# First norm by halves of the channels, two column tiles begun between the halves, and silu(c) rows by an identity product

## The chip, the cores and the metric

The kernel runs on one core of one Trainium2 chip. The metric is the device time of one execution in microseconds. TensorE (PE in the rows; PEld is its weight load), VectorE (DVE), ScalarE (ACT), GpSimd (POOL) and SyncE (SP, which issues most DMAs) each run their own queue of instructions in order.

## The reference

Two layers of a decoder trunk on 256 tokens of 1024 channels, in float32. What matters here is the head of each layer:

```python
mod = silu(c) @ w_ada[l] + b_ada[l]                    # 1024 -> 6 x 1024
sh1, sc1, gate_mix, sh2, sc2, gate_ffn = split(mod, 6)
h = rms_norm(x, norm_g[l, 0]) * (1.0 + sc1) + sh1
p = h @ w_in[l] + b_in[l]                              # 1024 -> 5144 columns
```

The columns of `p` feed an RWKV-7 time mix of 8 heads and a sparse attention of 8 heads; both are merged, projected and added to `x` with `gate_mix`. A second modulated norm (`sh2`, `sc2`) feeds a grouped top-2 mixture of 16 experts of width 512, added to `x` with `gate_ffn`.

## The kernel before

Activations lie transposed: `xT` holds 8 tiles of 128 channels by 256 tokens. The program is traced in Python, and a list scheduler orders each engine's queue at compile time by the order of tracing (the priority) and by its own estimate of when inputs are ready; on the chip each queue then runs in that fixed order, with semaphores.

**Start.** Ahead of the loop over layers, `x`, the vectors `v` and the constants' identity matrix are loaded. `cs` = silu(c) as a column of 8 per partition, `csx` its copy repeated 32 times. The sum of squares of `x` goes through ScalarE (L302), VectorE (L304) and TensorE (L307) to 1/rms (L245, L185), and `rs_rows` (L259) spreads it to rows in PSUM with a product against the identity. Then four pieces of the modulation of layer 0 are made in the order `ci` = 2, 0, 3, 1 (2 and 3 are the halves of `sc1`, 0 and 1 those of `sh1`): two weight tiles of 1 MB each (L313, `load` at L160) from a pool of eight, 8 products (16 instructions, L315), a copy by ScalarE (L318), four small products that sum the partitions back to a column (L321) and the sum with the bias (L322).

**Norm.** `norm_gain` makes `G` = (1 + sc1) * g in two operations (L252), and `norm_apply` goes over the 8 channel tiles: VectorE multiplies `xT`, `G` and the rows (L268), ScalarE adds the shift and rounds to the high part `h2[0]` (L269), VectorE makes the low part `h2[1]` (L270).

**Projection.** The input projection goes by column tiles of 128. `proj` takes a weight tile from a ring of three (`wcol`, 256 columns, so two column tiles each), splits its 1024 floats per partition into a high part (ScalarE, L274) and a low part (VectorE, L275), in one of two pairs of buffers, and `mm3` (L288) makes 24 products: for each channel tile high x high and low x high, then high x low. ScalarE takes the sum out of PSUM twice (L415, L417), and VectorE mixes it with the token before (L418). The tiles (0, 0) and (0, 128) come first, then those of the head pairs (`channels`, from weight tile 1 on).

**Rest of the mixing part.** The steps of the RWKV heads, the attention and the remaining modulation follow in a list written by hand (`STEPS`). The remaining modulation pieces (8 of this layer and 4 of the next) are reductions on VectorE: each of four operations per piece multiplies a loaded tile `wa` (L223) with `crow`, the row silu(c) in every partition, and sums (L225). `crow` is loaded in each layer, broadcast over the partitions, behind the first column tile; four pieces of it go through ScalarE (L431) and GpSimd (L432, L433).

**Experts.** 192 expert weight tiles of 1 MB in all are loaded through rings whose buffers come free as the mixing part and the experts before them finish. In layer 1 the rows of 1/rms come from the end of layer 0's experts, and the first half of the modulation is there already.

**Constants.** The rest of the constants `C` and the mask table `R` are loaded behind the modulation: a one-element copy from `mod` into the tile (L325, L355) holds the load back.

## Time and profile before

| | |
|---|---|
| timed runs | 1196.70, 1196.71, 1189.70 us; median 1196.7 |
| profiled execution | 1189.87 us, of which the span of the profile is 1188.1 |
| busy | PE 1068.4, PEld 688.4, DVE 653.2, ACT 402.8, POOL 134.1 us |
| TensorE clock granted, mean of the span | 0.959 |
| HBM read | 325.98 MB, 275 GB/s over the span |

Times in rows are microseconds from the start of the span, unless marked ns. The profiled execution's own time is longer than its span by what lies around the span.

### The profile page before, as it was taken

How to read it: one execution, taken by the hardware profiler on the slowest of the kernel's cores; microseconds unless marked ns; L12 is line 12 of the kernel's file. 1: busy time of each engine (PE TensorE's matmuls, PEld its weight loads, DVE VectorE, ACT ScalarE, POOL GpSimd, SP SyncE). 2: the span in 40 equal slices, each digit the busy share in tenths (PEclk: the TensorE clock that was granted, in tenths of full speed). 3: DMA queues.
4: the chain of work that ended last, by engine and by line, in shares of the span. 5: the costliest groups of instructions: out<-in, count | busy, mean ns of one | idle time of the engine just before them, and what ended most of it. 6: DMA issues, size and time to landing. Idle time of an engine off the chain costs nothing. (4 is left out here: it accounts for less than half of the span.)

```text
span 1188.1 us, 19652 instructions
## 1 busy us (share of the span) xinstructions
PE 1068.4 (90%) x7568; PEld 688.4 (58%) x7568; DVE 653.2 (55%) x1727; ACT 402.8 (34%) x922; POOL 134.1 (11%) x196
## 2 busy tenths in 40 slices
PE   5779899998797999999968999999989799999996
PEld 2658767886696343333337777778769744333432
DVE  1799788788575322121238988886748532212222
ACT  1634434356553020101035444344655321120100
POOL 0431232310000000000023212331000000000000
PEclk9889999999798999999988899999999899999998
DMA  9755664474577999999775466433346969999991
GB/s 382 266 189 187 224 226 174 168 245 164 200 311 321 373 421 419 420 420 419 295 268 179 152 239 213 161 135 133 108 167 273 409 267 420 420 420 419 419 396 38
DMA packets 52815, 328.48 MB, mean 276 GB/s; under 512 B 5856, under 2 KB 7520, under 8 KB 18784
## 3 DMA queue, kind: packets, MB, share of 16 engines
q1 hardware_dynamic: 52416, 326.91, 70.5%
q8 instruction: 63, 1.03, 0.3%
q14 instruction: 48, 0.39, 0.1%
q10 hardware_dynamic: 288, 0.14, 0.0%
HBM read 325.98 MB, written 1.05 MB: 275 GB/s over the span
## 5 line engine op out<-in xcount | busy, mean ns | idle before, releaser
L288 PE MATMUL ps_mm<-h,w 128*128 128x256 f32 x1824 | 266.8, 295 | 16.4 <-ACT w L274 8.1
L288 PEld LDWEIGHTS ps_mm<-h,w 128*128 128x128 f32 x1824 | 233.5, 194 | 35.7 <-issue 10.1
L275 DVE TENSOR_TENSOR w<-w,w 128x1024 fp32r<-128x1024 f32 (+2 forms) x130 | 140.2, 1082 | 16.3 <-ACT w L274 16.1
L274 ACT ACTIVATE w<-w 128x1024 fp32r<-128x1024 f32 (+2 forms) x130 | 120.1, 936 | 61.4 <-PE ps_mm L288 36.7
L1353 PE MATMUL ps_mm<-w,xeA 128*64 128x512 f32 x512 | 130.1, 599 | 0.0
L1364 PE MATMUL ps_mm<-w,hb 128*64 128x512 f32 (+1 forms) x576 | 123.0, 607 | 1.7 <-DMA w<-in_exp 1.2
L225 DVE CUSTOM_DVE_ANT_0 wa<-wa,crow 128x1024 f32<-128x1024 f32 x80 | 98.3, 1229 | 1.2 <-DMA wa<-in_ada 1.0
L1353 PE MATMUL ps_mm<-w,xeB 128*32 128x512 f32 (+1 forms) x640 | 97.8, 595 | 0.0
L275 DVE TENSOR_TENSOR ys<-ps_mm,ys 128x512 fp32r<-128x512 f32 x28 | 19.2, 686 | 110.5 <-ACT ys L274 110.5
L1364 PEld LDWEIGHTS ps_mm<-w,hb 128*64 128x64 f32 (+1 forms) x576 | 36.6, 127 | 73.3 <-issue 66.3
L737 PE MATMUL ps_mm<-w,h 128*128 128x512 f32 (+1 forms) x288 | 76.2, 394 | 1.0 <-DVE w L275 0.7
L1353 PEld LDWEIGHTS ps_mm<-w,xeA 128*64 128x64 f32 x512 | 37.5, 137 | 65.6 <-issue 62.3
L1307 DVE SCALAR_TENSOR_TENSOR hb<-hb,ps_mm 128x256 f32<-128x256 f32 x28 | 11.8, 421 | 99.7 <-ACT hb L1306 99.7
L274 ACT ACTIVATE ys<-ps_mm 128x512 fp32r<-128x512 f32 x28 | 16.7, 596 | 131.2 <-PE ps_mm L1364 101.3
L1308 DVE SCALAR_TENSOR_TENSOR hb<-ps_mm,sw,hb 128x256 f32<-128x256 f32 x28 | 12.3, 480 | 86.5 <-PE ps_mm L1353 86.5
L1329 DVE SCALAR_TENSOR_TENSOR xT<-ps_rw,gfh,xT 128x256 f32<-128x256 f32 x112 | 46.6, 478 | 23.3 <-PE ps_rw L1326 23.3
L1353 PEld LDWEIGHTS ps_mm<-w,xeB 128*32 128x32 f32 (+1 forms) x640 | 26.0, 115 | 51.8 <-issue 48.4
L737 PEld LDWEIGHTS ps_mm<-w,h 128*128 128x128 f32 x288 | 48.1, 198 | 12.5 <-issue 2.7
L1326 PEld LDWEIGHTS ps_rw<-ohT,ys 128*128 128x128 f32 x224 | 30.6, 188 | 38.8 <-ACT ys L274 19.4
L1243 PEld LDWEIGHTS ps_rw<-OH,h 128*128 128x128 f32 x256 | 35.7, 208 | 29.7 <-issue 23.8
L288 PE MATMUL ps_mm<-y,w 128*128 128x256 f32 x384 | 49.8, 294 | 3.2 <-ACT w L274 3.0
L288 PEld LDWEIGHTS ps_mm<-y,w 128*128 128x128 f32 x384 | 48.9, 200 | 3.9 <-ACT w L274 3.8
(458 smaller groups left out, 1512.9 us busy)
## 6 DMA issues: line engine op xcount, KB each, us to landing
w<-in_exp SPq DMA_DIRECT2D x192, 1024.0 KB, 19.7
w<-in_win SPq DMA_DIRECT2D x40, 1024.0 KB, 4.9
wa<-in_ada SPq DMA_DIRECT2D x80, 512.0 KB, 4.5
w<-in_ada SPq DMA_DIRECT2D x8, 1024.0 KB, 14.1
w<-in_cmp SPq DMA_DIRECT2D x8, 1024.0 KB, 6.0
w<-in_up SPq DMA_DIRECT2D x8, 1024.0 KB, 7.1
w<-in_out SPq DMA_DIRECT2D x8, 1024.0 KB, 5.9
row<-in_row SPq DMA_DIRECT2D x2, 780.0 KB, 7.3
```

Source lines behind the costliest of these rows:

```text
L225: ve.tensor_tensor_reduce(w, w, crow, 1.0, 0.0, op0=ALU.mult, op1=ALU.add, accum_out=mod[:, o:o + 1])
L274: ac.activation(hi, x, AF.Copy)
L275: e.tensor_sub(lo, x, hi.bitcast(F32))
L288: pe.matmul(out, lhsT=w2[i][:, k, :], rhs=x2[j][:, k, :], start=(k == ks[0] and not (i or j)), stop=(k == ks[-1] and j == 1), skip_group_c ...
L737: pe.matmul(p[tt][:, 0:n], lhsT=h2[j][:, k, tt * 128:tt * 128 + 128], rhs=w2[i][:, k - k0, :], start=(k == 0 and not (i or j)), stop=(k == ...
L1243: pe.matmul(p[:, k * 256:k * 256 + n], lhsT=h[:, tt, kk_ * 128:kk_ * 128 + 128], rhs=OH[:, tt, 0:n], start=(i == 0 and tt == 0), stop=(i = ...
L1307: ve.scalar_tensor_tensor(h[:, o], h[:, o], 1.0, p_g[:, o], op0=ALU.add, op1=ALU.mult)
L1308: ve.scalar_tensor_tensor(h[:, o], p_u[:, o], sw, h[:, o], op0=ALU.mult, op1=ALU.mult)
L1326: pe.matmul(p[:, i * 256:i * 256 + 256], lhsT=ys[:, n, o:o + 128], rhs=ohT, start=(n == 0), stop=(n == 1), skip_group_check=True)
L1329: ve.scalar_tensor_tensor(xT[:, d, :], p[:, i * 256:i * 256 + 256], gfh[:, d:d + 1], xT[:, d, :], op0=ALU.mult, op1=ALU.add)
L1353: pe.matmul(p[o:o + n, :], lhsT=xe[:, k, x:x + n], rhs=w[:, k % 4, :], start=(k == 0), stop=(k == NK - 1), skip_group_check=True)
L1364: pe.matmul(p2[n][o:o + m, :], lhsT=hsT[:, 2 * r + g, o:o + m], rhs=w[:, g, n * 512:n * 512 + 512], start=(r + g == 0), stop=(r + g == 2), ...
```

## The change

The pieces of the first modulation, the first norm and the first two column tiles are moved into the loop over layers, behind the opening of the pools, and are made by halves of the channels: for each half two modulation pieces (`sc1`, then `sh1`), four columns of `G`, four channel tiles of the norm, and for both column tiles of weight tile 0 the products of these four channel tiles. `begin` splits the weights once and keeps the PSUM tile open between the halves; `proj` uses a begun tile. Weight tile 0 is asked for ahead of the second half's modulation weights, weight tile 1 behind them, and then the two held loads of constants. The pool of modulation weights has five buffers in place of eight and lies on the other side of the memory. The modulation pieces no longer use the PSUM tiles `mm`, which the two column tiles hold.

`crow` is no longer loaded: `crow_rows` makes it in both layers with eight products of `cs`, repeated over 128 columns, against the identity matrix, and two copies by ScalarE. In layer 0 this stands ahead of the modulation pieces; in layer 1 ahead of the norm, with the copies held back behind the norm's last ScalarE operation.

```diff
@@ -245,12 +245,10 @@
         ve.tensor_scalar(ms, p[:, 0:2], 1.0 / D, 1e-6, op0=ALU.mult, op1=ALU.add)
         return rsqrt(ms, 2, tn)
 
-    def norm_gain(v, which, mod, sc0):
-        G = tn.tile([128, NK], F32, name="ng", tag="ng")
-        for i in (0, 4):
-            o = V_NG + 8 * which + i
-            ve.scalar_tensor_tensor(G[:, i:i + 4], mod[:, sc0 + i:sc0 + i + 4], 1.0, v[:, o:o + 4], op0=ALU.add, op1=ALU.mult)
-        return G
+    def norm_gain(v, mod, i, G):
+
+        o = V_NG + i
+        ve.scalar_tensor_tensor(G[:, i:i + 4], mod[:, 8 + i:12 + i], 1.0, v[:, o:o + 4], op0=ALU.add, op1=ALU.mult)
 
     def rs_rows(rs):
 
@@ -260,14 +258,22 @@
                       start=True, stop=True)
         return pr
 
-    def norm_apply(h2, pr, G, mod, sh0, room):
-
+    def norm_apply(h2, pr, G, mod, i, room):
+
+        for k in range(i, i + 4):
+            t = room[:, k - i]
+            sh = mod[:, k:k + 1]
+            ve.scalar_tensor_tensor(t, xT[:, k, :], G[:, k:k + 1], pr[:, 0:T], op0=ALU.mult, op1=ALU.mult)
+            persist["hi"] = ac.activation(h2[0][:, k, :], t, AF.Identity, bias=sh)
+            ve.scalar_tensor_tensor(h2[1][:, k, :], t, sh, h2[0][:, k, :].bitcast(F32), op0=ALU.add, op1=ALU.subtract)
+
+    def crow_rows(cs, tag):
+
+        p = [ps(tag), ps(tag)]
         for k in range(NK):
-            t = room[k // 4][:, k % 4]
-            sh = mod[:, sh0 + k:sh0 + k + 1]
-            ve.scalar_tensor_tensor(t, xT[:, k, :], G[:, k:k + 1], pr[:, 0:T], op0=ALU.mult, op1=ALU.mult)
-            ac.activation(h2[0][:, k, :], t, AF.Identity, bias=sh)
-            ve.scalar_tensor_tensor(h2[1][:, k, :], t, sh, h2[0][:, k, :].bitcast(F32), op0=ALU.add, op1=ALU.subtract)
+            pe.matmul(p[k // 4][:, 128 * (k % 4):128 * (k % 4) + 128], lhsT=cs[:, k:k + 1].to_broadcast([128, 128]), rhs=ident,
+                      start=True, stop=True)
+        return p
 
     def split(hi, lo, x, e=ve):
 
@@ -280,13 +286,13 @@
         split(wh, wl, w, e)
         return wh, wl
 
-    def mm3(out, w2, x2, ks=range(NK)):
+    def mm3(out, w2, x2, ks=range(NK), begin=True, end=True):
 
         for j in range(2):
             for k in ks:
                 for i in range(2 - j):
-                    pe.matmul(out, lhsT=w2[i][:, k, :], rhs=x2[j][:, k, :], start=(k == ks[0] and not (i or j)),
-                              stop=(k == ks[-1] and j == 1), skip_group_check=True)
+                    pe.matmul(out, lhsT=w2[i][:, k, :], rhs=x2[j][:, k, :], start=(begin and k == ks[0] and not (i or j)),
+                              stop=(end and k == ks[-1] and j == 1), skip_group_check=True)
 
 
     persist = {}
@@ -295,39 +301,26 @@
     sp.dma_start(xT, a["x"])
     cs = ada_begin(v)
     mod = lay.tile([128, 48], F32, name="mod", tag="mod", bufs=2)
-    with tc.tile_pool(name="start", bufs=8, reuse_waits="tile") as start:
...
-        persist["pr"] = rs_rows(norm_rs(pss))
-
-        for ci in (2, 0, 3, 1):
...
-    persist["mod"], persist["vec"] = mod, v
-
-    ve.tensor_copy(C[0:1, 128:129], mod[0:1, 0:1])
-    sp.dma_start(C[:, 128:], a["cst"][:, 128:NC])
+                pe.matmul(p[32 * j:32 * j + 32, :], lhsT=csx[:, 4 * r + j], rhs=w[:, 512 * j:512 * j + 512],
+                          start=(r == 0), stop=(r == 1), skip_group_check=True)
+        rows_ = start.tile([128, 512], F32, name="adar", tag="adar", bufs=2)
+        ac.activation(rows_, p, AF.Copy)
+        p = ps("rw")
+        for j in range(4):
+            pe.matmul(p[:, j:j + 1], lhsT=rows_[:, 128 * j:128 * j + 128], rhs=part32, start=True, stop=True)
+        ve.tensor_add(mod[:, ci * 4:ci * 4 + 4], p[:, 0:4], v[:, V_ADA + ci * 4:V_ADA + ci * 4 + 4])
 
     for l in range(layers):
         mod, v = persist["mod"], persist["vec"]
-        persist["pow0"] = persist["pow"]
+        persist["pow0"] = persist.get("pow")
         todo = [(l, ci, mod, v) for ci in range(4, 12)]
         if l + 1 < layers:
             mod2, v2 = lay.tile([128, 48], F32, name="mod", tag="mod", bufs=2), load_vec(l + 1)
@@ -351,9 +344,6 @@
                     for i in range(2)]
 
         R = lay.tile([128, NR_], F32, name="R", tag="R")
-        if l == 0:
-            ve.tensor_copy(R[0:1, 0:1], mod[0:1, 4:5])
-            sp.dma_start(R, a["cst"][:, NC:])
         row = wk.tile([128, NR], F32, name="row")
         mis = wk.tile([128, NM], F32, name="mis")
         w2a2 = mis[:, M_WA:M_WA + 512]
@@ -383,6 +373,51 @@
                 win[ci] = load("win", l, ci).rearrange("p (k n) -> p k n", k=4 if 8 <= ci < 12 else NK)
             return win[ci]
 
+
+        begun = {}
+
+        def begin(col, ks):
+            if col not in begun:
+                w2 = parts(NK, 128)
+                split(*w2, wcol(col[0])[:, :, col[1]:col[1] + 128])
+                begun[col] = ps("mm"), w2
+            p, w2 = begun[col]
+            mm3(p[:, 0:T], w2, h2, ks, ks[0] == 0, ks[-1] == NK - 1)
+            return p
+
+        G = tn.tile([128, NK], F32, name="ng", tag="ng")
+        crow = lay.tile([128, D], F32, name="crow", tag="crow")
+        if l == 0:
+            with tc.tile_pool(name="start", bufs=5, reuse_waits="tile", side="right") as start:
+                csx = start.tile([128, NK, 32], F32, name="csx", tag="csx", bufs=1)
+                ve.tensor_copy(csx, bc(cs.unsqueeze(2), [128, NK, 32]))
+                x2 = start.tile([128, NK, T], F32, name="x2", tag="x2", bufs=1)
+                ac.activation(x2, xT, AF.Square)
+                sq = start.tile([128, T], F32, name="sq", tag="sq", bufs=1)
+                ve.tensor_reduce(sq, x2.rearrange("p k t -> p t k"), axis=AX.X, op=ALU.add)
+                pss = ps("sq")
+                for tt in range(2):
+                    pe.matmul(pss[:, tt:tt + 1], lhsT=sq[:, tt * 128:tt * 128 + 128], rhs=ones[:, 0:1], start=True, stop=True)
+                pr = rs_rows(norm_rs(pss))
+                persist["pow0"] = persist["pow"]
+                for i, p in enumerate(crow_rows(cs, "mm")):
+                    ac.activation(crow[:, 512 * i:512 * i + 512], p, AF.Copy)
+                for half in range(2):
+                    if half:
+                        wcol(0)
+                    for n, ci in enumerate((2 + half, half)):
+                        ada0_piece(ci, mod, v, csx, ("sq", "rc")[n], start)
+                    norm_gain(v, mod, 4 * half, G)
+                    norm_apply(h2, pr, G, mod, 4 * half, x2[:, 4 * half:4 * half + 4])
+                    for col in ((0, 0), (0, 128)):
+                        begin(col, range(4 * half, 4 * half + 4))
+
+            wcol(1)
+            ve.tensor_copy(C[0:1, 128:129], mod[0:1, 4:5])
+            sp.dma_start(C[:, 128:], a["cst"][:, 128:NC])
+            ve.tensor_copy(R[0:1, 0:1], mod[0:1, 4:5])
+            sp.dma_start(R, a["cst"][:, NC:])
+
         NA = ExitStack()
         nka = NA.enter_context(tc.tile_pool(name=f"nka{l}", bufs=1, reuse_waits="tile", side="right"))
 
@@ -400,16 +435,19 @@
         def rp(shape, name, bufs=1, dt=F32):
             return rk1.tile([128] + shape, dt, name=name, tag=name, bufs=bufs)
 
-        norm_apply(h2, persist["pr"], norm_gain(v, 0, mod, 8), mod, 0, [rt([4, 256], "SC", 2) for _ in range(2)])
+        if l:
+            prow = crow_rows(cs, "rw")
+            for i in (0, 4):
+                norm_gain(v, mod, i, G)
+            for i in (0, 4):
+                norm_apply(h2, persist["pr"], G, mod, i, rt([4, 256], "SC", 2))
+            with tc.issue_after(persist["hi"].ins):
+                for i in range(2):
+                    ac.activation(crow[:, 512 * i:512 * i + 512], prow[i], AF.Copy)
 
         def proj(col, j, out):
 
-            ci, o = col
-            w = wcol(ci)
-            p = ps("mm")
-            w2 = parts(NK, 128)
-            split(*w2, w[:, :, o:o + 128])
-            mm3(p[:, 0:T], w2, h2)
+            p = begun[col][0] if col in begun else begin(col, range(NK))
             pb = rp([T + 1], "pb", 2)
             po.memset(pb[:, 0:1], 0.0)
             ac.activation(pb[:, 1:T + 1], p[:, 0:T], AF.Identity, bias=v[:, V_BIN + j:V_BIN + j + 1])
@@ -422,15 +460,6 @@
         if l:
             sp.dma_start(R, a["cst"][:, NC:])
         sp.dma_start(mis, a["mis"][l])
-
-        crow = lay.tile([128, D], F32, name="crow", tag="crow")
-        sp.dma_start(crow, a["c"].to_broadcast([128, D]))
-        for i in range(4):
-            t = rt([4, 64], "Xs", 2).rearrange("p c n -> p (c n)")
-            part = crow[:, 256 * i:256 * i + 256]
-            ac.activation(t, part, AF.Tanh, scale=0.5)
-            po.tensor_scalar(t, t, 0.5, 0.5, op0=ALU.mult, op1=ALU.add)
-            po.tensor_mul(part, part, t)
         TL = rp([T], "TL")
         ac.activation(TL[0:64], x12[0:64, :], AF.Tanh)
         ac.activation(TL[64:128], x12[64:128, :], AF.Copy)
```

## Rows read from the trace of the kernel before

**Rows 1.** The page, busy time of the span: engine, us, share, instructions.

```profile
PE 1068.4 (90%) x7568; PEld 688.4 (58%) x7568; DVE 653.2 (55%) x1727; ACT 402.8 (34%) x922; POOL 134.1 (11%) x196
```

**Rows 2.** Windows by stage: stretch, its length, busy by engine, PEclk, DMA share, GB/s.

```profile
47.00:336.00 289.00, 258.57 (x2244) 209.91 (x2244) 237.25 (x636) 136.11 (x326) 56.45 (x71) 0.95 0.56 197
...
400.00:580.00 180.00, 173.66 (x937) 67.35 (x938) 42.89 (x100) 26.51 (x58) 0.00 (x0) 1.00 1.01 420
```

**Rows 3.** Timeline, 0 to 31 us: start, length, instruction, then idle time before and releaser.

```profile
13.08 1.93 PE L315 MATMUL ps_mm<-w,csx 128*32 128x512 f32 x6
...
14.93 1.22 PE L259 MATMUL ps_tr<-C,rs 128*128 128x128 f32 x4
...
26.24 1.92 PE L315 MATMUL ps_mm<-w,csx 128*32 128x512 f32 x16
...
28.29 0.60 ACT L318 ACTIVATE adar<-ps_mm 128x512 f32<-128x512 f32 x1 [3.09 <-PE ps_mm L315]
...
28.94 1.05 PE L321 MATMUL ps_rw<-part,adar 128*128 128x1 f32 x8 [0.78 <-ACT adar L318]
30.03 0.16 DVE L322 TENSOR_TENSOR mod<-ps_rw,vec 128x4 f32<-128x4 f32 x1 [3.32 <-PE ps_rw L321]
```

**Rows 4.** Line 160 in the first 10 us: the loads of the modulation weights.

```profile
L160 SPq DMA_DIRECT2D w<-in_ada x8: 327/440/783, 1.6 to 7.1; - x8
...
DMA to landing us min/median/max: 7.4/14.1/19.4
```

**Rows 5.** Timeline, 31 to 54 us.

```profile
31.18 0.48 DVE L268 SCALAR_TENSOR_TENSOR SC<-xT,ng,ps_tr 128x256 f32<-128x256 f32 x1
...
31.65 0.87 DVE L268 SCALAR_TENSOR_TENSOR SC<-xT,ng,ps_tr 128x256 f32<-128x256 f32 x2
31.69 0.98 ACT L269 ACTIVATE h<-SC,mod 128x256 fp32r<-128x256 f32 x2 [2.80 <-DVE SC L268]
...
37.61 2.36 DVE L275 TENSOR_TENSOR w<-w,w 128x1024 fp32r<-128x1024 f32 x2
...
38.89 6.37 PE L288 MATMUL ps_mm<-h,w 128*128 128x256 f32 x34 [2.50 <-DVE w L275]
...
44.00 0.48 ACT L415 ACTIVATE pb<-ps_mm,vec 128x256 f32<-128x256 f32 x1 [1.51 <-PE ps_mm L288]
...
47.36 5.95 PE L288 MATMUL ps_mm<-h,w 128*128 128x256 f32 x48
```

**Rows 6.** Windows of the start, columns as in Rows 2.

```profile
0.00:9.00 9.00, 0.00 (x0) 0.00 (x0) 1.34 (x7) 3.40 (x3) 1.51 (x8) 1.00 0.79 295
...
33.70:38.90 5.20, 1.14 (x3) 0.55 (x3) 5.20 (x13) 4.09 (x9) 1.25 (x1) 0.50 0.94 367
...
43.80:46.80 3.00, 3.00 (x27) 2.87 (x25) 1.37 (x2) 2.66 (x6) 0.66 (x2) 1.00 1.00 383
```

**Rows 7.** Timeline, the norm of layer 1.

```profile
619.81 0.71 PE L259 MATMUL ps_tr<-C,rs 128*128 128x128 f32 x4 [1.03 <-POOL rs L185]
...
620.62 1.26 DVE L268 SCALAR_TENSOR_TENSOR SC<-xT,ng,ps_tr 128x256 f32<-128x256 f32 x3 [1.42 <-issue]
...
622.59 2.86 DVE L270 SCALAR_TENSOR_TENSOR h<-SC,mod,h 128x256 fp32r<-128x256 f32 x3
...
623.19 0.72 POOL L433 TENSOR_TENSOR crow<-crow,Xs 128x256 f32<-128x256 f32 x1
...
629.88 0.47 DVE L270 SCALAR_TENSOR_TENSOR h<-SC,mod,h 128x256 fp32r<-128x256 f32 x1
...
631.47 0.48 ACT L415 ACTIVATE pb<-ps_mm,vec 128x256 f32<-128x256 f32 x1 [2.11 <-PE ps_mm L288]
```

**Rows 8.** Windows of layer 1's begin, columns as in Rows 2.

```profile
619.80:621.70 1.90, 0.72 (x5) 0.53 (x5) 1.08 (x3) 0.57 (x2) 1.90 (x4) 0.67 0.96 390
```

**Rows 9.** Line 223, 40 to 60 us: loads of the modulation reductions, issue to landing.

```profile
DMA to landing us min/median/max: 5.7/8.6/9.3
```

**Rows 10.** Timeline, the first modulation reduction.

```profile
57.47 1.22 DVE L225 CUSTOM_DVE_ANT_0 wa<-wa,crow 128x1024 f32<-128x1024 f32 x1
```

More of the change, by code (lines that the diff above doesn't have):

```diff
@@ L323, in tile_trunk, with ada0_piece @@
-    persist["mod"], persist["vec"] = mod, v
-    ve.tensor_copy(C[0:1, 128:129], mod[0:1, 0:1])
-    sp.dma_start(C[:, 128:], a["cst"][:, 128:NC])
+    persist["mod"], persist["vec"] = mod, v
+    def ada0_piece(ci, mod, v, csx, tag, start):
+        p = ps(tag)
+        for r in range(2):
+            w = load("ada0", ci, r, pool=start)
+            for j in range(4):
+                pe.matmul(p[32 * j:32 * j + 32, :], lhsT=csx[:, 4 * r + j], rhs=w[:, 512 * j:512 * j + 512],
[6 more added lines that the diff above has]
+        ve.tensor_add(mod[:, ci * 4:ci * 4 + 4], p[:, 0:4], v[:, V_ADA + ci * 4:V_ADA + ci * 4 + 4])
```

20 lines of the change are left out of this document (removed).

## The prediction, made before the change was run

> **What bounds the kernel now.** I read the busy totals of the page first, then the windows by stage, then the timeline of the first 47 us and of the stretch in which layer 1 begins. The totals say little: TensorE is busy 90% of the span [rows 1]. By stage, the mixing part of layer 0 (47 to 336 us) keeps TensorE busy for 258.57 of 289 us and VectorE for 237.25, so whatever lets both begin earlier should end earlier too; in the expert part (400 to 580 us) the DMA rings move 420 GB/s without a break [rows 2]. The expert loads are issued as buffers of the mixing part come free, so that part moves with its start. What the change touches is neither stage but the 47 us ahead of them.
>
> There the reader is to see one chain. The last of the four modulation pieces is multiplied from 26.24, copied by ScalarE at 28.29, turned by TensorE at 28.94, and its sum with the bias ends at 30.19 [rows 3]. The last weight of these pieces was issued at 7.1 and landed 19.4 later, at 26.5 [rows 4]: from the landed weight to the finished modulation 3.7 us pass. Only now does the norm begin: VectorE at 31.18, then sixteen operations of 0.435 us (0.87 for two), the low parts of the first two column tiles from 37.61, and TensorE's products in earnest at 38.89. ScalarE takes the first product out of PSUM at 44.00; that frees the buffers for the split of the third column tile, whose products start at 47.36 [rows 5]. TensorE's clock is at 0.50 from 33.7 to 38.9, behind a stretch without products, and at 1.00 from 43.8 on [rows 6].
>
> **The change part by part.** *Order of the loads.* The first weight tile of the input projection (128 x 2048 floats, 1.05 MB) is now issued ahead of the second half's modulation weights instead of behind everything. The last modulation weight waits for that much more: 2.5 us at the 420 GB/s of [rows 2]. The modulation then ends at 30.19 + 2.5 = 32.7 if DMA bounds it. The pool of these weights has five buffers in place of eight, so the sixth to eighth load wait for TensorE to free a tile. The first tile's products end near 15 us, because the sum of squares stands between them [rows 3]; by then three of the seven tiles issued have not landed, so I cost this wait at nothing. A later release than that would cost its own length.
>
> *First half of norm and products.* Eight of the sixteen norm operations (3.5 us), both splits (2.36 us on VectorE) and half of the 48 products move into the time in which the second half's weights arrive. VectorE has little more there than a sum of 0.16 us per piece [rows 3], so on VectorE they cost nothing. On TensorE they need room. A piece takes 3.7 us (26.24 to 29.99 [rows 3]), so the first half's modulation is done two pieces before 30.19, near 22.8, and the last weight lands near 29.0. In these 6.2 us TensorE does the products of one piece and its turn (1.92 + 1.05 us) and 24 products, 3.0 us at the full clock (48 in 5.95) and up to 4.9 at the rate of the first two tiles (34 in 6.37, with some waits) [rows 5]. That is 6.0 to 7.9 us, an overflow of 0 to 1.7; I take 0.3, near the full clock, as TensorE has just been busy.
>
> *What remains behind the modulation.* A gain operation of 0.16 us, eight norm operations of 0.435, ScalarE's 0.49 between them [rows 5]: the last low part is ready some 3.9 us after the modulation. The first column's last products follow it, and those that need no low part are done before. It is out between 4.2 us (full clock) and 1.1 + 4.9 = 6.0 us (half clock, both columns mixed) after the modulation; I take 4.5, since VectorE sets the pace. So 32.7 + 0.3 + 4.5 = 37.5 against 44.00 now: **6.5 us earlier**, with ends of 44.0 - (32.7 + 1.7 + 6.0) = 3.6 and 44.0 - (32.7 + 4.2) = 7.1. Next late is the split of the third tile, which needs its 3.4 us from the first eviction to its products [rows 5]; it moves with the chain, to 40.9.
>
> *Loads moved behind.* The later constants and the mask table now wait for the last piece, and stand behind the second weight tile. With the small tables behind them on SyncE's queue they are 416 + 1442 + 1504 columns of 128 floats, 1.7 MB, 4 us at the rate above, so about 39 us. Their first readers stand behind the first column's eviction, at about the same time. Behind the waiting issue stands the third weight tile too, wanted by the fifth column tile, some 6 us after the third. I cost this at 0, at most 1.
>
> *Rows of silu(c).* Removed in each layer: a 512 KB load, four ScalarE operations, eight on GpSimd. Added: eight products of 128 columns and two ScalarE copies of the 0.60 us form [rows 3]. The nearest products have the same shape and are two instructions each: four instructions take 1.22 us in layer 0 [rows 3] and 0.71 in layer 1 [rows 7], so the sixteen 2.9 to 4.9. In layer 0 TensorE does nothing in the first 9 us [rows 6], and the inputs need only the first small loads: cost 0; if they came behind the sum of squares, up to 4.9 of TensorE's time, of which the next piece's wait for its weights would hide most.
>
> *Layer 1.* There the norm begins at 620.62, and its last operation ends at 630.35: 9.7 us against 16 x 0.435 = 7.0. Three of its operations took 2.86 us, where three others took 1.26, while GpSimd was making the rows [rows 7], and a modulation reduction was put before the last. Without GpSimd the norm ends near 627.6; the first product would be out 0.4 later, but the two copies (1.2 us) are ordered in front of its eviction on ScalarE: 629.2 against 631.47, 2.2 earlier. Against that, two modulation reductions of 1.22 [rows 10] that VectorE had done by then are still owed, and the sixteen identity instructions must fit into TensorE's idle time, 1.2 us of the 1.9 in [rows 8] and some ahead of it: up to 2 us. So from 2.2 later (nothing of the norm gained) to 2.2 earlier; I take **1 us earlier**, as the owed reductions fall where VectorE also waits.
>
> The sum is 6.5 + 1.0 = 7.5 us: 1189.87 - 7.5 = 1182.4 for an execution like the profiled one. The three timed runs are 1196.70, 1196.71 and 1189.70: the profiled execution stands on the lower of two levels 6.9 us apart, the median on the upper. No row says which one a run takes, so I add half the distance: **1186 us**.
>
> **The rivals.** (a) *The lead isn't carried.* VectorE, busy for 237 of 289 us in a fixed order, could give up the lead in waits elsewhere. For it: no engine is full in [rows 2]. Against it: both are nearly so, and nothing else starts that stage. A gain of 1 to 2 us: 1192. (b) *Slower: reductions of the modulation move ahead of their data.* With the rows of silu(c) ready in the first 9 us, the order written at compile time can put the first reductions ahead of splits that TensorE waits for. Their loads landed 5.7 to 9.3 us after their issue [rows 9], and the first of them ran at 57.47 [rows 10]. If VectorE stands 9.3 us at one and does four (4.9 us) first, the 7.5 are more than lost: 6.7 slower, 1200. It decides where a reduction comes ahead of the third tile's split; against it speaks that they now come 10 us behind that tile's products. (c) *More.* The same early rows let VectorE fill some of the 52 us in which it idles in the mixing part with four reductions that then need not be done later: 7.5 + 5 = 12.5, and 1181. (d) *The halves don't do what they say*: products in short groups between waits run at half clock, as they do once in the rows, 0.50 behind an idle TensorE [rows 6]. With both bounds above at their slow ends the gain is 3.6, and layer 1 gives nothing: 1190. [...]
>
> **How the numbers follow.** Forecast 0.47; (a) 0.18; (b) 0.10; (c) 0.13; (d) 0.12. Each case has both levels of the runs, so it spreads 3.4 us either way. The low end of the range is (c) on the lower level, 1177.4, and 1 for its size: 1176. The high end holds (a) on the upper level, 1195.2, and the lower part of (b): 1198. A measurement of this kernel can tell about 1% (12 us) from no change. Faster by more than that, against the median of 1196.7, means under 1184.7: the forecast on the lower level (0.235), (c) on both (0.13) and a little of the rest, 0.39. Slower by over 1% needs more than (b) gives: 0.08. Within 1%: 0.53.
>
> **What would show it.** Right: products of the two column tiles between 23 and 30 us; the last modulation sum near 33; the first eviction of a projection near 37.5 and the third tile's products near 41; identity products in the first 9 us; in layer 1 a norm of about 7 us on VectorE with no GpSimd beside it; an expert part that begins 5 to 8 us earlier. Wrong: a last modulation sum past 35, a clock of 0.5 in both groups, a reduction waiting for its load ahead of the third tile's products, or an expert part that begins where it does now.

## The result: slower by 1.3%, and the profile after

The changed kernel took 1208.7 us (median of six, 1204.69 to 1213.8), the kernel before 1193.4 in the runs beside it: ratio 1.0128, 95% interval 1.009 to 1.0166. That is 15.3 us slower where 7.5 us faster was worked out, and outside the range. The profiled execution after took 1213.8 us, the slowest of its six, the one of before 1189.87, near its fastest. So the two traces lie 24 us apart where the medians lie 15 apart; what is read from them is where time goes, and how much is taken from the timed runs of the experiments.

The page after, busy time of the span of 1211.9 us [rows 1 for before]: TensorE has 22.9 us more, VectorE 2.7 less, GpSimd 16.2 less.

```profile
PE 1091.3 (90%) x7600; PEld 705.6 (58%) x7600; DVE 650.5 (54%) x1727; ACT 402.9 (33%) x918; POOL 117.9 (10%) x180
```

The timeline of the start (start, length, instruction, idle time before it and what released it):

```profile
3.83 3.44 PE L274 MATMUL ps_mm<-C,cs 128*128 128x128 f32 x16 [3.83 <-DVE cs L216]
...
24.29 1.70 ACT L267 ACTIVATE h<-x,mod 128x256 fp32r<-128x256 f32 x4 [1.41 <-DVE mod L319]
...
25.90 1.99 ACT L280 ACTIVATE w<-w 128x1024 fp32r<-128x1024 f32 x2
...
26.99 0.39 PE L294 MATMUL ps_mm<-h,w 128*128 128x256 f32 x1 [3.00 <-ACT w L280]
...
27.94 5.38 PE L294 MATMUL ps_mm<-h,w 128*128 128x256 f32 x23 [0.56 <-ACT w L280]
...
33.25 2.31 PE L312 MATMUL ps_sq<-w,csx 128*32 128x512 f32 x16
...
37.32 1.92 PE L312 MATMUL ps_rc<-w,csx 128*32 128x512 f32 x16
...
37.83 1.66 DVE L266 SCALAR_TENSOR_TENSOR x<-xT,ng,ps_tr 128x256 f32<-128x256 f32 x4
...
41.11 0.16 DVE L319 TENSOR_TENSOR mod<-ps_rw,vec 128x4 f32<-128x4 f32 x1 [1.63 <-PE ps_rw L318]
...
41.87 3.10 PE L294 MATMUL ps_mm<-h,w 128*128 128x256 f32 x24 [0.79 <-ACT h L267]
...
44.18 0.48 ACT L453 ACTIVATE pb<-ps_mm,vec 128x256 f32<-128x256 f32 x1 [1.17 <-PE ps_mm L294]
```

The sixteen identity products (L274) lie in the empty first 9 us, as expected. The two halves are there too: 24 products of the first one (L294) from 26.99, 24 of the second from 41.87. But between them stand both pieces of the second half of the modulation (L312 at 33.25 and 37.32). In TensorE's queue the first half's products were put ahead of the third piece; they waited 3.00 us for ScalarE's splits (L280, behind its four h operations), and the piece began at 33.25, where the last of them ends (27.94 + 5.38). The last modulation sum ends at 41.27 instead of 30.19 [rows 3], the first eviction comes at 44.18 instead of 44.00, the third tile's products at 47.47 instead of 47.36 [rows 5]. The start gained nothing.

Windows of the same start (stretch, length, TensorE busy and products, granted clock, DMA share, GB/s): the first group of products ran at half clock (0.54 and 0.50), behind 3.00 us without products, the second at the full clock (1.00).

```profile
24.00:27.00 3.00, 0.01 (x1) 1.00 1.02 423
27.00:30.00 3.00, 2.44 (x10) 0.54 1.01 421
30.00:33.00 3.00, 3.00 (x16) 0.50 0.79 325
...
42.00:45.00 3.00, 2.98 (x24) 1.00 0.83 277
```

The norm of layer 1, columns of the timeline: GpSimd makes no rows beside it (it has 2.23 us of memsets there, the last one ending at 630.32), and no modulation reduction stands among its operations.

```profile
628.09 1.26 DVE L266 SCALAR_TENSOR_TENSOR SC<-xT,ng,ps_tr 128x256 f32<-128x256 f32 x3 [1.42 <-issue]
...
629.27 1.27 DVE L268 SCALAR_TENSOR_TENSOR h<-SC,mod,h 128x256 fp32r<-128x256 f32 x3
...
633.88 0.89 DVE L268 SCALAR_TENSOR_TENSOR h<-SC,mod,h 128x256 fp32r<-128x256 f32 x2 [0.19 <-ACT h L267]
...
635.86 0.48 ACT L453 ACTIVATE pb<-ps_mm,vec 128x256 f32<-128x256 f32 x1 [0.64 <-PE ps_mm L294]
```

The three operations that took 2.86 us [rows 7] take 1.27, and the norm 6.7 us (628.09 to 634.77) in place of 9.7.

Where the rest went is seen by setting the start of the same instruction in both traces side by side. Lag against the profiled execution of before, in us (KC and KZ are the writes of two key tiles of the attention, KC near the begin of a mixing part, KZ some 90 us ahead of its end; the second norm ends it; e1, e2 and so on are the experiments below, where "old order" means the instruction order of before):

```
                            before    after  e1: layer 1   e9: both    e2: rows   e4: behind   e7: mended  e8: mended
                              at             old order     old order   only       pieces       start       old order
last modulation sum           30.0    +11.1     +11.4       +10.3       +0.4        +8.2        +0.1        +2.5
first eviction                44.0     +0.2      +1.4        +0.4       +0.6        -2.1        -3.9        -1.6
layer 0, KC                   95.0     +0.3      -0.7        +0.7       +1.9        -4.9        -7.5        -1.9
layer 0, KZ                  253.3     +2.4      +0.6        +4.9       +1.7        -2.9        -3.3        -0.7
layer 0, second norm         347.6     +6.6      +3.0        +5.1       +5.1        +0.4        -2.5        -0.2
layer 1, sum of squares      618.8     +7.5      +5.2        +5.3       +7.5        +0.7        -2.0        +0.1
layer 1, KC                  677.3     +6.5      +5.1        +2.4       +5.1        -1.4        -3.3        -2.6
layer 1, KZ                  828.8    +21.4      +5.1        +2.5      +16.1        +9.1        +6.0        -2.6
last instruction            1187.7    +23.9      +6.3        +2.2      +17.6       +10.1        +7.3        -3.0
```

In the changed kernel layer 0 loses 6.3 us from KC to the second norm, and layer 1 loses 14.9 from KC to KZ, although the diff touches no line of either stretch. The order of their instructions on each engine is written at compile time, and an edit of what stands ahead can deal it anew. That is theory S; its rival W is that the changed work itself costs the time.

The traces show the orders themselves. From KC to KZ of layer 1 only two occur, the same on all engines: that of before (in before, e1, e3, e5, e6, e8, e9, and, but for the added sums, e10 to e13) and one other (in the changed kernel, e2, e4 and e7, the kernels with the new rows of silu(c) and no fixed order). In layer 0 each kernel whose order isn't fixed there has one of its own; e1 has that of the changed kernel.

In layer 1's mixing part the loss can be read from TensorE. Windows of the changed kernel (stretch, length, busy time and products of TensorE, PEld, VectorE, ScalarE, GpSimd, then the granted clock, DMA share, GB/s):

```profile
684.00:722.00 38.00, 36.67 (x452) 29.03 (x451) 32.74 (x95) 16.19 (x36) 5.56 (x13) 1.00 0.67 232
722.00:736.00 14.00, 12.26 (x130) 8.44 (x133) 8.85 (x21) 6.72 (x15) 6.65 (x8) 0.92 0.40 130
736.00:754.00 18.00, 17.09 (x93) 12.40 (x86) 13.20 (x36) 5.78 (x15) 1.98 (x3) 0.78 0.65 229
754.00:790.00 36.00, 35.72 (x300) 25.07 (x300) 29.89 (x80) 14.69 (x35) 11.07 (x12) 1.00 0.42 145
790.00:812.00 22.00, 20.04 (x164) 16.04 (x162) 14.38 (x41) 6.22 (x12) 4.54 (x8) 0.69 0.34 125
```

TensorE stands idle for 1.7 of the 14 us from 722; its granted clock is 1.00 ahead of them, 0.92 in them and 0.78 in the 18 us that follow. From 754 it is 1.00 again, and from 790, with 2.0 of 22 us idle, 0.69. Over the whole part, from KC to KZ, the kernel before and the changed one (TensorE alone):

```profile
677.20:828.80 151.60, 145.44 (x1457) 1.00 0.52 180
```
```profile
683.90:850.40 166.50, 158.52 (x1478) 0.93 0.48 166
```

A mean clock of 0.93 over 166.5 us is some 11.7 us of full-clock time not granted, 8.0 us idle against 6.2 add 1.8: 13.5 of the 14.9 us. The other order also holds 24 more projection products in this stretch, some 3 us at the full clock (24 took 3.10 in the start, at 1.00); nothing of the lag is made good behind KZ. The same stretch in e1 and e5, with the order of before, and in e2, with the other:

```profile
682.60:834.20 151.60, 145.32 (x1457) 1.00 0.51 179
```
```profile
697.10:851.70 154.60, 148.41 (x1456) 0.98 0.51 176
```
```profile
682.40:844.80 162.40, 153.72 (x1474) 0.96 0.48 170
```

All runs fit this. With the order of before, KC to KZ took 151 to 152 us at a mean clock of 1.00 in before, e1, e3, e6, e8, e9, and 154.6 at 0.98 in e5; with the other order 160.8 at 0.97 in e7, 162.1 at 0.96 in e4, 162.4 at 0.96 in e2, 166.5 at 0.93 in the changed kernel.

What in the other order makes the clock fall is not shown. The longest wait of TensorE is no longer in it than in before, where one of 1.3 us passes at a clock of 1.00 (what waited for what, us in total, times, longest; before, then the changed kernel):

```profile
PE ps_rc L696 <- DVE adx L693: 1.8, 2, 1.3
```
```profile
PE ps_rc L725 <- DVE adx L722: 1.9, 2, 1.1
```

### The profile page after: what moved, and what is told of

Its sections match the earlier page's. It is cut to its first block, busy times and chain, and to the rows that moved or that the text cites. A ratio compares the mean times of both kernels' runs of the same rounds, so it can differ in the third digit from the quotient of the medians.

```text
span 1211.9 us, 19716 instructions
## 1 busy us (share of the span) xinstructions
PE 1091.3 (90%) x7600; PEld 705.6 (58%) x7600; DVE 650.5 (54%) x1727; ACT 402.9 (33%) x918; POOL 117.9 (10%) x180
## 5 line engine op out<-in xcount | busy, mean ns | idle before, releaser
L294 PE MATMUL ps_mm<-h,w 128*128 128x256 f32 x1824 | 267.1, 295 | 13.8 <-DVE w L281 7.5
L294 PEld LDWEIGHTS ps_mm<-h,w 128*128 128x128 f32 x1824 | 234.1, 194 | 34.2 <-DVE w L281 11.6
L280 ACT ACTIVATE w<-w 128x1024 fp32r<-128x1024 f32 (+2 forms) x130 | 119.9, 936 | 67.2 <-PE ps_mm L294 38.0
L766 PE MATMUL ps_mm<-w,h 128*128 128x512 f32 (+1 forms) x288 | 82.5, 417 | 3.8 <-DVE w L281 3.5
L766 PEld LDWEIGHTS ps_mm<-w,h 128*128 128x128 f32 x288 | 52.0, 212 | 15.0 <-DVE w L281 3.9
L280 ACT ACTIVATE ys<-ps_mm 128x512 fp32r<-128x512 f32 x28 | 16.7, 597 | 131.9 <-PE ps_mm L1393 109.6
L294 PE MATMUL ps_mm<-y,w 128*128 128x256 f32 x384 | 51.4, 298 | 4.1 <-ACT w L280 3.8
L294 PEld LDWEIGHTS ps_mm<-y,w 128*128 128x128 f32 x384 | 49.9, 204 | 5.3 <-ACT w L280 5.3
L1272 PEld LDWEIGHTS ps_rw<-OH,h 128*128 128x128 f32 x256 | 35.5, 207 | 29.0 <-issue 23.8
```

Source lines behind the costliest of these rows:

```text
L280: ac.activation(hi, x, AF.Copy)
L294: pe.matmul(out, lhsT=w2[i][:, k, :], rhs=x2[j][:, k, :], start=(begin and k == ks[0] and not (i or j)), stop=(end and k == ks[-1] and j = ...
L766: pe.matmul(p[tt][:, 0:n], lhsT=h2[j][:, k, tt * 128:tt * 128 + 128], rhs=w2[i][:, k - k0, :], start=(k == 0 and not (i or j)), stop=(k == ...
L1272: pe.matmul(p[:, k * 256:k * 256 + n], lhsT=h[:, tt, kk_ * 128:kk_ * 128 + 128], rhs=OH[:, tt, 0:n], start=(i == 0 and tt == 0), stop=(i = ...
```

## The experiments

**e1. The changed kernel, layer 1's mixing part in the order of before.** The instructions are the same; their order on each engine is fixed by dependencies that make no engine wait for another.

```
+        pin(tc, l, list(tc.nc.cur_bb.bb.instructions)[mark:])
...
+        for x, y in zip(order, order[1:]):
+            tc.add_manual_dep(mine[y], mine[x].name,
+                              mybir.DependencyInfo(mybir.DependencyClass.NoSync, mybir.DependencyReason.DATA), reason="pin")
```

> The changed kernel, with the instruction order of all five engines in layer 1's mixing part (2415 instructions, from the first LoRA activation to the end of the merges) forced to the order that the kernel before has there; the work is the changed kernel's. Theory S (the 17 us that layer 1 loses between 640 and 900 us come from another order written at compile time): layer 1's mixing part takes its old length, so about 1208.7 - 17 = 1192, with layer 0 as in the changed kernel. Theory W (they come from the changed work itself, the rows of silu(c) made by TensorE and ScalarE, or their time of readiness): about 1208, as the changed kernel.

Measured: 1195.06 us, ratio 1.0001 (0.9968 to 1.0035). From KC to KZ of layer 1 the lag stays at 5.1 us instead of growing by 14.9. Order alone, with nothing else undone, gives back the whole difference that the timed runs show. S holds for layer 1. It is not the profiled execution alone: over all timed executions the median granted clock is 0.953 in the changed kernel and 0.961 in e1, which over their spans (1206.8 and 1193.2 us) is 10 of the 13.6 us between them.

**e2 and e3. One part of the change alone.** e2: only the rows of silu(c) by identity products (the load, four ScalarE and eight GpSimd operations removed in each layer). e3: only the halves, with the rows of silu(c) made as before.

```
-            po.tensor_scalar(t, t, 0.5, 0.5, op0=ALU.mult, op1=ALU.add)
-            po.tensor_mul(part, part, t)
...
+            pe.matmul(p[k // 4][:, 128 * (k % 4):128 * (k % 4) + 128], lhsT=cs[:, k:k + 1].to_broadcast([128, 128]), rhs=ident,
+                      start=True, stop=True)
```

> The kernel before with one part of the change: the rows of silu(c) by identity products in both layers. Theory W(rows): slower by most of the 15 us. Theory S: the start as before (first eviction near 44.0), layer 1's norm 2 us shorter as in the changed kernel, and the mixing parts longer or shorter by as much as a new order gives, within 10 us of 1193 either way, with no single place where the rows cost more than 1 us.

> The changed kernel with the rows of silu(c) loaded and made by ScalarE and GpSimd as before. Theory H (TensorE's queue holds the first half's products in front of the second half's pieces): first eviction still near 44 us, no lead at 47 us. Theory W(rows): back to about 1193. Theory S: 1193 to 1210, wherever its order falls.

Measured: e2 1209.33 us, ratio 1.0148 (1.0084 to 1.0212); e3 1201.65, ratio 1.0064 (1.0038 to 1.009). The rows, costed at nothing in layer 0, cost as much alone as the whole change does. By the time alone this is what W(rows) said, and more than the 10 us that S allowed; e6 decides. e2 is 5.1 us late at the second norm of layer 0, and loses 10.9 us from KC to KZ of layer 1, in the same order as the changed kernel. e3 has its first eviction at 45.18, as H says; it loses 7.5 us between KC and KZ of layer 0 and nothing there in layer 1, where its order is that of before.

**e4. The first half's products queued behind the second half's piece products.** To test whether the place in TensorE's queue (theory H) is what cost the start its lead.

```
+                    if half:
+                        with tc.issue_after(persist["piece"].ins):
+                            for col in ((0, 0), (0, 128)):
+                                begin(col, range(4))
...
-                    for col in ((0, 0), (0, 128)):
-                        begin(col, range(4 * half, 4 * half + 4))
+                for col in ((0, 0), (0, 128)):
+                    begin(col, range(4, 8))
```

> The changed kernel with the first half's products of both column tiles queued on TensorE behind the products of the second half's pieces. Theory H: the last modulation sum moves from 41.3 to about 33 us and the first eviction from 44.2 to 37 to 39, a lead of 5 to 7 us at 47 us. If H is wrong and the loads or the five buffers held the pieces back, they stay near 41 and 44. In total, 6 us less than 1208.7 if the rest keeps its length (1203); by theory S the rest is dealt anew, 1190 to 1210.

Measured: 1205.88 us, ratio 1.0107 (1.0055 to 1.0159). The third piece now goes at once (25.92), but its copy (L315) stands on ScalarE behind the splits (L280), TensorE idles 2.58 us for it, and the fourth piece's sixteen products take 3.64 us where they took 1.92. The timeline of e4:

```profile
25.92 1.92 PE L312 MATMUL ps_sq<-w,csx 128*32 128x512 f32 x16
...
27.90 1.99 ACT L280 ACTIVATE w<-w 128x1024 fp32r<-128x1024 f32 x2
...
29.79 0.58 ACT L315 ACTIVATE adar<-ps_sq 128x512 f32<-128x512 f32 x1
30.42 1.87 PE L318 MATMUL ps_rw<-part,adar 128*128 128x1 f32 x8 [2.58 <-ACT adar L315]
...
32.22 3.64 PE L312 MATMUL ps_rc<-w,csx 128*32 128x512 f32 x16
```

So H is right on TensorE (the piece runs 7.3 us earlier than in the changed kernel, which also shows that its weights had landed), and the same holds on ScalarE: two queues held the pieces, not one. The last sum ends 2.9 us earlier only, at 38.4 where about 33 was expected, and the first eviction comes at 41.95, not at 37 to 39.

**e5. A control: the kernel before with five start buffers in place of eight.**

```
-    with tc.tile_pool(name="start", bufs=8, reuse_waits="tile") as start:
+    with tc.tile_pool(name="start", bufs=5, reuse_waits="tile") as start:
```

> The kernel before with one number changed: five buffers instead of eight for the modulation weights. No work is added, removed or moved in the program text. Theory S (a new order written at compile time costs by itself): the start stays within 1 us of the kernel before, but the compiler deals the queues anew (some 870 lines of VectorE's order differ), and the total moves by several us, up to 15 either way, in the mixing parts. If orders cost little and the losses of the other runs came from their work: 1194, within 2.

Measured: 1206.29 us (1200.27 to 1212.33), ratio 1.0103 (1.0058 to 1.0149). It isn't as neutral as it was meant: its profiled execution, the slowest of the four, has a modulation that ends 8.1 us late. Behind the first piece none waits for its load there; TensorE's products are slow (see the last section). But even its fastest run is 11.5 us over the fastest of before in that comparison (1188.75). Of the profiled execution's lag 9.6 us stand at KC of layer 0, 9.8 arise from there to the second norm, in a new order, and 3.1 between KC and KZ of layer 1, in the order of before, at a clock of 0.98. One number in a pool thus goes with about 1% of the time; how much of that is the new order of layer 0 and how much the slow start, one trace can't tell.

**e6. The rows of silu(c) alone, both mixing parts in the order of before.** e2 with the fixed order of e1, for both layers (e8 and e9 have it in the same way).

```
+        pin(tc, l, list(tc.nc.cur_bb.bb.instructions)[mark:])
```

> The rows of silu(c) by identity products on top of the kernel before (as in the run with the rows only, 1209), with the order of the kernel before forced on all engines in the mixing parts of both layers. Theory S: the 15 us go away, and what remains is the rows' own effect, layer 1's norm some 2 us shorter and layer 0 unchanged: 1190 to 1193. Theory W(rows): 1205 to 1209.

Measured: 1193.75 us, ratio 1.0016 (0.9992 to 1.0041). The 15 us of e2 are gone (S gave 1190 to 1193, W 1205 to 1209); the rows cost nothing that can be measured.

**e7 and e8. The start mended, without and with the old order.** The modulation weights all first (eight buffers, the first weight tile behind them), the first half's products behind the last turn of the modulation, and the first piece in another PSUM tile.

```
-            with tc.tile_pool(name="start", bufs=5, reuse_waits="tile", side="right") as start:
+            with tc.tile_pool(name="start", bufs=8, reuse_waits="tile", side="right") as start:
...
+                    for n, ci in enumerate((2 + half, half)):
+                        ada0_piece(ci, mod, v, csx, ("rc", "sq")[n], start)
                     if half:
-                        wcol(0)
-                    for n, ci in enumerate((2 + half, half)):
-                        ada0_piece(ci, mod, v, csx, ("sq", "rc")[n], start)
+                        with tc.issue_after(persist["turn"].ins):
+                            for col in ((0, 0), (0, 128)):
+                                begin(col, range(4))
```

> The changed kernel with its start mended: eight buffers again, the first weight tile of the projection loaded behind all modulation weights, the first piece in the PSUM tile that the sum of squares does not use, and the first half's products queued on TensorE behind the last piece's turn. Theory H: last modulation sum near 30 us, first eviction of a projection at 35.5 to 37, a lead of 7 to 8 us at 47 us. The compiler's own order follows in the mixing parts, so by theory S the total is anywhere from 1180 to 1205.

> The mended start, with the order of the kernel before forced on all engines in the mixing parts of both layers. Theories H and S together: the lead of the start (7 us) and of layer 1's norm (2 us) are carried to the end: 1194 - 9 = 1185. If the mixing part has slack of its own that takes up the lead (rival a of the prediction): 1190 to 1193.

Measured: e7 1203.08 us, ratio 1.0096 (1.0064 to 1.0127); e8 1188.12, ratio 0.9985 (0.9959 to 1.0011). The timeline of e7:

```profile
30.15 0.16 DVE L319 TENSOR_TENSOR mod<-ps_rw,vec 128x4 f32<-128x4 f32 x1 [1.63 <-PE ps_rw L318]
...
33.60 7.87 PE L294 MATMUL ps_mm<-h,w 128*128 128x256 f32 x47 [0.36 <-ACT w L280]
...
40.09 0.48 ACT L455 ACTIVATE pb<-ps_mm,vec 128x256 f32<-128x256 f32 x1 [6.14 <-PE ps_mm L294]
```

The modulation ends on time, the first eviction comes 3.9 us earlier, and KC of layer 0 7.5 us earlier: a lead of the forecast's size can be had. The eviction at 40.09 misses the expected 35.5 to 37: TensorE waits 2.5 us for the splits and then has a clock of 0.50 from 33 to 36. e7 loses the lead in its own order, 5.0 us of it from KC to the second norm of layer 0 and 9.3 from KC to KZ of layer 1. With the old order e8's lag stays between +0.1 and -3.0 us from the first eviction on; its profiled start had a lead of only 1.6. Its time lies between the 1185 of H and S and the 1190 to 1193 of rival (a) and decides neither. e8 has the lowest median of all kernels here and is faster than the changed one by 20 us, but whether it beats the kernel before is not settled by its interval.

**e9. The changed kernel, both mixing parts in the order of before.**

> The changed kernel with the mixing parts of both layers in the order of the kernel before, on all five engines; the start (halves, five buffers, products in front of the pieces) is left as changed. Theory S (what costs the time is the order that was dealt anew): the last modulation sum still ends some 11 us later than before and the first eviction some 0.4 to 2 us later, but nothing more is lost between 253 and 299 us or in layer 1's mixing part; layer 1's norm gives its 2 us. So 0 to 2 us against before: 1190 to 1195, ratio 0.998 to 1.002. TensorE's granted clock is 1.00 throughout 684 to 830 us. Theory W (the changed start itself costs it, by a lead that VectorE owes later): the 5 to 8 us between 253 and 299 are lost in this order too, 1198 to 1202, ratio 1.005 to 1.008.

Measured: 1191.8 us (1185.39 to 1203.45), ratio 0.9975 (0.9941 to 1.0009), within the 1190 to 1195 of S. The start is as late in it as in the changed kernel (last sum +10.3), so all that the change measurably costs is the order; W falls. The loss between 253 and 299 us that both theories speak of can't be used: it was read at the product of the router weights with their gain on VectorE, which the changed kernel's order puts later in the queue. Its lag there is +9.4, that of VectorE's operation just ahead in before +3.0.

All traces support S in layer 0 too. From KC to the second norm the kernels with an order of their own there lose 3.2 to 9.8 us (the changed one, e1 to e5, e7), those with the order of before 0.1 to 1.7 (e6, e8, e10 to e13), and e9 4.4 (last section).

**e10 to e13. What in an order costs the time.** The kernel before in its own fixed order, with sums that nobody reads added on VectorE directly ahead of L693, for which TensorE waits in layer 1's mixing part: one of 512 columns, one of 2048, one of 2048 with a stride, two of these. The edit of the last two (the count is 1 or 2):

```
+        for k in range(1 * l):
+            extra.append(ve.tensor_reduce(tn.tile([128, 16], F32, name="wt", tag="wt", bufs=1), xT.rearrange("p k (s t) -> p t (k s)", t=16),
+                                          axis=AX.X, op=ALU.add).ins)
```

> The kernel before in its own order (both layers pinned to it), with one operation added on VectorE in layer 1's mixing part, a sum over 512 columns (about 0.95 us) whose result nobody reads, directly ahead of the operation of line 693 at 720.5 us, for which TensorE's products of line 696 wait. Theory C (a wait of TensorE costs more than its length, because the granted clock falls behind it): TensorE waits some 0.8 us there, the clock falls to 0.50 for some us, and the stretch to the end of the mixing part at 829 us is 2 to 4 us later. Theory L (a wait costs its length at most): 0 to 1 us later, the clock stays at 1.00. Either way the time stands within 4 us of before, ratio 0.999 to 1.004: the trace tells them apart.

> As the short wait, with a sum over 2048 columns (about 3.6 us) at the same place. Theory C: TensorE waits some 3 us, the granted clock falls to 0.50 behind that, and the end of the mixing part is 5 to 8 us later; the later waits that this brings cost clock again. Theory L: at most 3.6 us later, less what later idle time takes up, with the clock at 1.00. Time by C 1197 to 1202, ratio 1.004 to 1.008; by L 1193 to 1197, ratio 1.000 to 1.003.

> As the long wait, but the added sum on VectorE, at the same place ahead of line 693, takes its 2048 columns with a stride (2.3 to 3.6 us, by the rows of the long wait and of the first sum of squares): TensorE should wait 0.8 to 2.1 us there. Theory C (the clock falls behind such a wait): the clock is at 0.50 for some us after it, the end of the mixing part (829 us before) comes 3 to 6 us later. Theory L (a wait costs its own length at most): 0.7 to 2.1 us later, the clock at 1.00. Time by C 1195 to 1200, ratio 1.002 to 1.006; by L 1193 to 1196, ratio 0.999 to 1.002.

> Two of these sums in a row at the same place: TensorE waits some 3 to 6 us. Theory C: the clock falls to 0.50 behind this wait, and 2 to 4 us are lost beyond the wait: the end of the mixing part 6 to 10 us later, ratio 1.005 to 1.009. Theory L: at most the wait's own 3 to 6 us, less what the later idle time of 5.5 us in that part takes up, with the clock at 1.00: ratio 1.001 to 1.005. If the clock falls here and not in the run with one sum, TensorE's time without work, not the order itself, is what it follows.

Measured: the added sums took 0.68, 2.28, 3.60 and 7.20 us; TensorE waited 0, 0.82, 2.11 and 5.71 us for line 693; the lag from KC to KZ grew by -0.3, 0.7, 4.2 and 7.7 us. The clock stayed at 1.00 for the first two and fell for the other two, to 0.56 and 0.58 in the 6 us from 726. TensorE's wait in e11:

```profile
724.07 0.44 PE L790 MATMUL ps_rc<-C,adx 128*128 128x128 f32 x2 [0.82 <-DVE adx L787]
```

In e12, the wait in the timeline, then the windows around it (TensorE busy, granted clock, DMA share, GB/s):

```profile
724.96 0.69 PE L790 MATMUL ps_rc<-C,adx 128*128 128x128 f32 x2 [2.11 <-DVE adx L787]
```
```profile
714.00:720.00 6.00, 6.00 (x79) 1.00 0.54 182
720.00:726.00 6.00, 3.89 (x48) 0.87 0.53 175
726.00:732.00 6.00, 6.00 (x40) 0.56 0.00 0
732.00:738.00 6.00, 6.00 (x45) 1.00 0.65 214
```

Windows of e13:

```profile
720.00:726.00 6.00, 2.01 (x25) 1.00 0.40 144
726.00:732.00 6.00, 4.28 (x18) 0.58 0.00 0
732.00:738.00 6.00, 6.00 (x47) 0.85 0.28 87
```

In e12's trace a wait of 2.11 us cost 4.2: 0.13 x 6 + 0.44 x 6 = 3.4 us of full-clock time are missing behind it, and about 1.3 of the 5.5 is absorbed later. In these traces theory C holds at 2.11 us and not at 0.82; in e13 the wait itself is most of the cost. The times are 1192.52, 1193.74, 1192.87 and 1199.81 us, ratios 1.0002 (0.9967 to 1.0036), 1.0 (0.9967 to 1.0032), 0.9975 (0.9946 to 1.0004) and 1.0064 (1.0033 to 1.0095). Only e13 can be told from no change, and its interval, 3.9 to 11.3 us, holds the wait's own 5.7 as well as the 7.7 of the trace. Single executions of before spread over 12 us, so the 4 us of e12 are seen in its trace and not in its median, which lies below what either theory gave. Its profiled execution also has the lowest mean clock of its ten, 0.955 against 0.957 to 0.961: the fall behind 2.11 us is shown for one execution, and may not come in each. e10, in which TensorE didn't wait, tells nothing of C and L, but shows that fixing the order of before costs nothing that can be measured.

## Why the prediction was wrong

Two steps failed: the start gained nothing, and the mixing parts did not keep their time. The first took the forecast gain away, the second made the 15 us of loss.

*The overflow, "0 to 1.7; I take 0.3".* This step failed. The weights came as forecast: the last tile landed at 28.97 (29.0). The room on TensorE was summed (6.0 to 7.9 us of work in 6.2), but not the order of the queue. The third piece could have followed the turn that ends at 23.99 and began at 33.25, 9.3 us later: 3.0 for the splits, the rest for 24 products at some 0.23 us each. These were priced near the full clock, 3.0 us, "as TensorE has just been busy"; it had just been idle for the splits, 3.00 us, and they took 5.77 at 0.54 and 0.50. (The upper bound of 4.9 is not what its rows give: 24 at 34 in 6.37 are 4.5.) In the rows above the third piece begins where the products ahead of it end: the question to ask was not whether the products fit, but when the first of them has its operands. The test named in the prediction, a last modulation sum past 35, showed it: 41.27.

*What remains behind the modulation, 4.5 us.* It took 2.9 (41.27 to 44.18), better than either end. Four of the eight norm operations (L266) need only the third piece and ran from 37.83, ahead of the last sum; the sum had put all eight behind it. So 1.6 us were regained here of the 8.3 by which the modulation missed its 33.0: a lead of -0.2 us, not 6.5.

*The five-buffer wait, at nothing.* The eighth load was issued at 21.4 in place of 7.1 [rows 4], but behind the first piece none of the changed kernel or of e5 waited for its weights. Right, as far as the waits go.

*The rows of silu(c), 0 in layer 0.* Right as a cost (e6), and misleading as a forecast: with the order that they brought, they moved the time by 15 us (e2).

*Layer 1, 1 us earlier.* Right. The lag falls from 7.5 at the sum of squares to 5.7 at the tanh behind the first column, and stands at 6.5 at KC, with the reductions still owed: 1.0 us. In the old order (e9) it is 2.8.

*The rivals.* (a) had no lead to lose; e7, which had 7.5 us at KC of layer 0, keeps 2.5 of it at the second norm. (b), reductions ahead of their data, didn't happen: the first came at 68.48 in place of 57.47 [rows 10]. (c) didn't happen either. (d) was half right: the first group of 24 products took 5.77 us (0.39 + 5.38), the second 3.10, at the full clock. The rival had both at half clock. The first stood behind 3.00 us of idle time, for ScalarE, and had 0.54 and 0.50; the second stood behind 0.79 and had 1.00.

*"That part moves with its start": what no case held.* This step failed too, and it holds most of the miss. Each case let the mixing parts keep the time they had, and moved them as a block. That of layer 0 alone is 289 us long [rows 2], and a new order of the two is worth more than any term of the sum: 16.9 us between the changed kernel and e9, 15.6 between e2 and e6, 15.0 between e7 and e8. Of the changed kernel's, 13.6 us go with layer 1's order (1208.7 to 1195.06), good to a few us, as it is a difference of medians; the 3.3 with layer 0's (to 1191.8) can't be told from nothing by the two intervals. Of layer 1's loss the path is shown: with the other order TensorE's granted clock is lower, in each of its four traces. What in that order lowers it is open, as the waits in it are hardly longer. In layer 0 the clock doesn't tell the orders apart: from KC to the second norm it is 0.96 in the changed kernel and 0.97 in before. Why these orders lose time there, and why the compiler wrote them, is open.

## What to carry to other kernels

Before an operation is moved ahead of a wait, read on every engine's queue what will stand behind it, and cost the wait for its operands there, not its busy time (here the third piece began 9.3 us late). Where an order is written at compile time, an edit has two effects, what it does and the new order of everything behind it; measure the first with the old order fixed, and put the spread of the second (here about 1%) into every forecast. Compare the orders themselves, not only the times: an edit can leave one layer's order as it was and deal the other's anew. And set lags by operations that stand at the same place in both queues. And look behind a wait of TensorE, in a part that it bounds, for more than its length: in one trace (e12) 2.11 us cost 4.2, with a granted clock of 0.56 in the 6 us behind it.

## What was not expected of the hardware

One and the same order had a fall of the clock in one execution and none in another. e9, in layer 0's mixing part (TensorE busy, granted clock, DMA share, GB/s), where before has 1.00 from 95 to 253 us:

```profile
156.00:162.00 6.00, 5.17 (x52) 0.66 0.80 298
162.00:168.00 6.00, 6.00 (x46) 0.50 0.61 209
```

e9 loses 4.2 us by KZ there, while the waits of TensorE in that part are the same in both (2.1 us for adx, 1.9 for iG). That is of the size by which executions of one kernel differ. e5 did the same from KC to KZ of layer 1: 3.1 us longer at 0.98, in an order that has 1.00 in six other traces.

And products were slow while the granted clock read 1.00. In e5 sixteen products of a piece took 3.64 us, which took 1.92 in before [rows 3]; first the timeline, then the window:

```profile
20.37 3.64 PE L315 MATMUL ps_mm<-w,csx 128*32 128x512 f32 x16
...
26.52 3.64 PE L315 MATMUL ps_mm<-w,csx 128*32 128x512 f32 x16
```
```profile
18.00:36.00 18.00, 15.93 (x72) 1.00 0.77 289
```

e8 shows the same until 23.4 us (3.56 us for the second piece) and not after (1.92). At 3.64 us a piece is as slow as in e4, where the clock reads 0.57 to 0.50. e7 and e8 have the same start, and the modulation ends at 30.3 in the one and 32.7 in the other by this alone. What sets it is not shown.
